# Pinning the matmuls of the 1024-column gemms in the order in which the kernel names them

## The chip, the cores and the metric

One core of a Trainium2 chip runs the whole kernel. The metric is the device time of one launch in microseconds, as the median of several runs. TensorE (PE) multiplies, VectorE (DVE) and ScalarE (ACT) prepare operands and read results out of PSUM, SyncE (SP) and GpSimd (POOL) issue the loads.

## The reference

Two transformer blocks, one after the other, on 256 tokens of width 2048 in float32. Cut to the large products:

```
# first block
h = rmsnorm(x, norm_attn); proj = h @ w_in
ya = dilated_attention(...); yb = rmsnorm(diff_attention(...))
x = x + concatenate([ya, yb]) @ w_out                      # "wo1" in the kernel
h = rmsnorm(x, norm_ffn)
x = x + (silu(h @ w_gate) * (h @ w_up)) @ w_down           # "wgu", "wd"
x = rmsnorm(x, norm_final)
# second block
z = rmsnorm(x, norm1_g) @ w_in
a_out = forgetting_attention(...)                          # "fox"
m_out = rmsnorm(mlstm_chunkwise(...)) * sigmoid(...)
merged = sigmoid(g_a) * (a_out @ w_proj_a) + sigmoid(g_m) * (m_out @ w_proj_m)   # gates: "wgs"
x = x + merged @ w_out                                     # "wo2"
u = causal_dwconv(rmsnorm(x, norm2_g) @ w_up)
x = x + (silu(u_gate) * u_val) @ w_down                    # "wd2"
```

## The kernel before

Every float32 operand is cut into a high and a low part in fp32r. Activations lie in SBUF as pairs of parts (class Pair: hi, lo), weights are loaded as 1024-column raw tiles and cut by `split` (L80): ACT casts the high part wh (L83), DVE subtracts to get the low part wl (L84). Both have four buffers, so the split of a tile waits until PE has done with the tile four before it. One product of a 128x128 piece of activations with 512 columns of weights is three matmuls, high by high, high by low, low by high, in `mm3` (L133; its matmul is L136).

`gemm` (L192) makes 256 x 1024 results in four PSUM banks c[t][col], with t the half of the tokens and col the half of the columns. It does not issue work at once: it makes a list `todo` of closures (loads, cuts, products) and runs them in order at the end. Two kinds of stage fill the list. A Plain stage takes two weight tiles; `part(h)` names, for one of them, twelve matmuls: for each 512-column half and each half of the tokens one product of three matmuls, so each goes to another of the four banks. The last Plain stage of a gemm (`by_bank`) names all products of one bank before those of the next. A Seven stage does a 2x2 block by Strassen's scheme with seven products into p1, p5, p6, p7 and c; it has four cuts (w0 to w3, of raw tiles and of the sums ta and tb) and names its products in three steps, `one` (p1, c01, c00), `two` (p5, p7, from ta) and `three` (p6, c10, from tb), between which a Plain stage's parts 0 and 1 stand. `chain` (L316) folds p1, p5, p6 and p7 together on ACT and DVE (s1 at L317, u2 at L318 and so on).

PSUM has four banks with the tag "d" and four with "a". c is in "d", except in the second wo1 gemm, where it is in "a"; p1, p5, p6 and p7 are in "a", and so are the scores of the attention (L574), the transposed probabilities (L581), the value products (L603) and the transposes of results (`turned`, L374), which DVE and ACT read out as pairs (`put`, L113 and L114; `put2`, L118 and L119).

What sets the order: the kernel names its work in one sequence, and a scheduler of the framework reorders each engine's instructions by the data they need and by times that it expects. A matmul given to `tc.keep_in_program_order` may not pass the PE instruction that was named just before it. Before the change `mm3` gets that wish only from `by_bank` of a gemm that was called with `ends` (the last one of the kernel). wo1's, wgu's, wd's, wgs's, wo2's and wd2's products go through `gemm`; the other projections (`xstat`, `wstat`), attention and transposes do not, and are never pinned.

Of the kernel before, what the change touches and what calls it, by code (L numbers as in the profile page):

```python
# [57 lines left out]
def body(ctx: ExitStack, tc: tile.TileContext, xT, xn, gfr, gp, cst, rst, w1, wo1, wgu, wd,  # L58
# [11 lines left out]
    def raw_tile(src):  # L70
        t = rp.tile([P, 1024], F32, tag="raw", name="raw")
        n = src.shape[-1]
        nc.sync.dma_start(t[:, :n], src)
        return t
# [6 lines left out]
    def split(src, n, eng=dve):  # L81
        wh, wl = wtiles()
        act.copy(wh[:, :n], src)  # L83
        eng.tensor_sub(wl[:, :n], src, wh[:, :n].bitcast(F32))  # L84
        return wh, wl

    def bank(tag="a"):
        t = psp.tile([P, 512], F32, tag=tag, name=tag)
        return t
# [44 lines left out]
    def mm3(ps, ah, al, wh, wl, start, stop, pin=False):  # L134
        for i, (a, b) in enumerate(((ah, wh), (ah, wl), (al, wh))):
            m = pe.matmul(ps, a, b, start=start and i == 0, stop=stop and i == 2)  # L136
            if pin:
                tc.keep_in_program_order(m)
# [53 lines left out]
    def gemm(srcs, xs, n_sum, fold=None, mid=None, tag="d", tail=1, lead=0, last=((0, 0), (0, 1), (1, 0), (1, 1)), ends=False):  # L192
# [13 lines left out]
        todo, count, done = [], {}, {}  # L206

        def mm(ps, lhs, w, o, pin=False):
            count[id(ps)] = count.get(id(ps), 0) + 1

            def go():
                k = done[id(ps)] = done.get(id(ps), 0) + 1
                wh, wl = w[0][:, o:o + 512], w[1][:, o:o + 512]
                mm3(ps, *lhs(), wh, wl, k == 1, k == count[id(ps)], pin)
            todo.append(go)

        def later(f):
# [2 lines left out]
        class Seven:  # L220
# [17 lines left out]
            def lhs(self, n):  # L238
                pr = xs[self.i]
                return (pr.s[:, 0, n], pr.s[:, 1, n]) if n < 4 else (pr.a(0, (n - 4) % 2, (n - 4) // 2),  # L240
                                                                     pr.a(1, (n - 4) % 2, (n - 4) // 2))
# [267 lines left out]
    with tc.tile_pool(name="a1", bufs=1) as ap1:  # L509
# [131 lines left out]
        for grp in range(4):  # L641
# [18 lines left out]
            else:  # L660
# [7 lines left out]
                for h in range(4):  # L668
                    for t in range(2):
                        dve.tensor_scalar_mul(on[:, t, h, :], on[:, t, h, :], ss[:, t, h:h + 1])  # L670
                    ps = bank()
# [87 lines left out]
    with tc.tile_pool(name="a2", bufs=1) as ap2:  # L759
# [105 lines left out]
        for w in (wmq, wmk):  # L865
            m = n4("mT")[:, 0:1024].rearrange("p (h s) -> p h s", h=4)
            for j in range(4):
                ps = bank()
# [44 lines left out]
        for j in range(4):  # L913
# [3 lines left out]
            for hf in range(2):  # L917
                ps = bank()
# [77 lines left out]
    with tc.tile_pool(name="mg", bufs=8) as mp:  # L996
        for b in range(4):
# [8 lines left out]
            for i in (1, 0):  # L1006
                for q in range(2):
                    for h in range(2):
                        wh, wl = split(raw_tile(wpr[b][i][q][:, h * 1024:(h + 1) * 1024]), 1024)
                        for kk in range(2):  # L1010
                            k = 4 * q + 2 * h + kk
# [197 lines left out]
```

## Time and profile before

| what | value |
|---|---|
| median of 3 runs | 2508.8 us (2508.21 to 2511.95) |
| the profiled execution | 2509.22 us |
| its span in the profile | 2507.4 us |
| granted TensorE clock, mean | 0.999 |
| PE, DVE, ACT busy | 2496.5, 1829.8, 1386.3 us |

In a row of the profile "d<-wh,x" means that a PSUM bank with the tag d is written from weights wh and activations x; the number after it is the tile's shape. Matmuls are pipelined, so the span of one (0.39 us for 512 columns) is longer than the distance from one start to the next.

### The profile page before, as it was taken

Reading aid. Unit: us, or ns where it says so; the run is one execution under the profiler, and the core shown is the slowest. Engines: PE = TensorE matmul, PEld = TensorE weight load, DVE = VectorE, ACT = ScalarE, POOL = GpSimd, SP = SyncE. Lnnn points to the kernel's source line nnn. Section 1 sums busy time; section 2 is a strip of 40 time slices with the busy share of each in tenths; the row PEclk is TensorE's granted clock in tenths of the full one; section 3 lists DMA queues with packets and bytes.
Section 4 is the critical chain, followed back from the end, with each engine's and each line's share of the span. In section 5 each row is a group of like instructions: output and inputs, shape, how many; then the busy total and the mean of one; then the engine's idle time right before and its main releaser. Section 6 shows DMA issues by size and latency. Waiting matters only on the chain.

```text
span 2507.4 us, 32737 instructions
## 1 busy us (share of the span) xinstructions
PE 2496.5 (100%) x11977; PEld 2080.4 (83%) x11977; DVE 1829.8 (73%) x2538; ACT 1386.3 (55%) x1943; POOL 74.1 (3%) x81
## 2 busy tenths in 40 slices
PE   9999999999999999999999999999999999999999
PEld 7888888888888888887888888888888888888887
DVE  6666567899888888886565555455788887878787
ACT  6555455665555555575456544444655555555554
POOL 0000000000000000000000000000000000000000
PEclk9999999999999999999999999999999999999999
DMA  8445566889888888866544456555756755685665
GB/s 328 151 152 170 172 203 203 255 249 271 263 250 257 259 257 246 264 199 201 189 156 160 161 191 193 192 190 186 233 189 202 249 188 186 209 260 187 187 198 170
DMA packets 159186, 528.07 MB, mean 211 GB/s; under 512 B 16688, under 2 KB 16944, under 8 KB 158768
## 3 DMA queue, kind: packets, MB, share of 16 engines
q1 hardware_dynamic: 148512, 488.75, 58.5%
q0 software_dynamic: 9936, 36.18, 8.0%
q8 instruction: 94, 1.54, 0.2%
q10 hardware_dynamic: 576, 1.05, 0.1%
q14 instruction: 68, 0.56, 0.1%
HBM read 523.81 MB, written 2.10 MB: 210 GB/s over the span
## 4 chain that ended last, share of the span: by engine, by line
PE 98%; DVE 1%; DMA 0%; issue 0%; ACT 0%; SPq 0%; DVEq 0%; ACTq 0%
PE d L136 60%; PE a L141 14%; PE a L136 12%; PE a L142 7%; PE a L374 1%; PE a L574 1%; DVE wl L84 0%; PE a L581 0%; PE d L141 0%; DMA xin<-in_xT 0%; PE a L633 0%; PE a L565 0%; PE a L603 0%; ACT wh L83 0%; PE d L142 0%
## 5 line engine op out<-in xcount | busy, mean ns | idle before, releaser
L84 DVE TENSOR_TENSOR wl<-raw,wh 128x1024 fp32r<-128x1024 f32 (+1 forms) x882 | 1037.3, 1181 | 550.1 <-ACT wh L83 546.7
L83 ACT CAST wh<-raw 128x1024 fp32r<-128x1024 f32 (+1 forms) x882 | 890.9, 1017 | 948.1 <-PE d L136 555.8
L136 PE MATMUL d<-wh,x 128*128 128x512 f32 x2932 | 926.8, 392 | 1.7 <-ACT wh L83 1.7
L136 PEld LDWEIGHTS d<-wh,x 128*128 128x128 f32 x2932 | 548.5, 188 | 115.2 <-ACT wh L83 2.8
L136 PE MATMUL d<-wl,x 128*128 128x512 f32 x1466 | 574.0, 392 | 0.9 <-DVE wl L84 0.9
L141 PE MATMUL a<-x,wh 128*128 128x512 f32 x1504 | 531.3, 399 | 0.0
L142 PE MATMUL a<-x,wl 128*128 128x256 f32 x1504 | 421.8, 281 | 0.0
L136 PE MATMUL d<-wh,y 128*128 128x512 f32 x1104 | 352.8, 391 | 0.2 <-ACT wh L83 0.2
L141 PEld LDWEIGHTS a<-x,wh 128*128 128x128 f32 x1504 | 282.4, 188 | 69.9
L136 PEld LDWEIGHTS d<-wl,x 128*128 128x128 f32 x1466 | 275.3, 188 | 59.8 <-DVE wl L84 2.9
L142 PEld LDWEIGHTS a<-x,wl 128*128 128x128 f32 x1504 | 284.1, 189 | 0.4
L136 PEld LDWEIGHTS d<-wh,y 128*128 128x128 f32 x1104 | 207.1, 188 | 43.8 <-ACT wh L83 0.6
L136 PE MATMUL d<-wl,y 128*128 128x512 f32 x552 | 213.4, 390 | 1.2 <-DVE wl L84 1.2
L136 PE MATMUL a<-wh,y 128*128 128x512 f32 x456 | 147.3, 390 | 0.4 <-ACT sv L392 0.4
L136 PEld LDWEIGHTS d<-wl,y 128*128 128x128 f32 x552 | 103.8, 188 | 23.6 <-DVE wl L84 2.0
L136 PEld LDWEIGHTS a<-wh,y 128*128 128x128 f32 x456 | 85.6, 188 | 18.9 <-ACT sv L392 0.6
L136 PE MATMUL a<-wl,y 128*128 128x512 f32 x228 | 88.6, 389 | 0.0
L84 DVE TENSOR_TENSOR wl<-ta,wh 128x1024 fp32r<-128x1024 f32 x69 | 84.2, 1221 | 4.8 <-ACT wh L83 4.6
L84 DVE TENSOR_TENSOR wl<-tb,wh 128x1024 fp32r<-128x1024 f32 x69 | 84.1, 1219 | 3.4 <-ACT wh L83 3.4
L136 PE MATMUL d<-wh,m 128*128 128x512 f32 x256 | 79.8, 391 | 0.0
L136 PE MATMUL a<-wh,sy 128*128 128x512 f32 x216 | 77.8, 393 | 0.0
L83 ACT CAST wh<-ta 128x1024 fp32r<-128x1024 f32 x69 | 72.6, 1051 | 8.8 <-PE d L136 3.9
(323 smaller groups left out, 2218.1 us busy)
## 6 DMA issues: line engine op xcount, KB each, us to landing
raw<-in_wup SPq DMA_DIRECT2D x176, 512.0 KB, 4.4
raw<-in_wgu SPq DMA_DIRECT2D x143, 512.0 KB, 6.3
raw<-in_wd SPq DMA_DIRECT2D x140, 512.0 KB, 5.5
raw<-in_w SPq DMA_DIRECT2D x95, 512.0 KB, 3.9
raw<-in_wo SPq DMA_DIRECT2D x64, 512.0 KB, 4.5
raw<-in_wgs SPq DMA_DIRECT2D x64, 512.0 KB, 4.3
raw<-in_wfox SPq DMA_DIRECT2D x48, 512.0 KB, 3.8
ta<-in_wd SPq DMA_DIRECT2D x36, 512.0 KB, 7.7
```

Source lines behind the costliest of these rows:

```text
L83: act.copy(wh[:, :n], src)
L84: eng.tensor_sub(wl[:, :n], src, wh[:, :n].bitcast(F32))
L136: m = pe.matmul(ps, a, b, start=start and i == 0, stop=stop and i == 2)
L141: pe.matmul(ps, wh, pr.t[:, :, j, :], start=start, stop=False)
L142: pe.matmul(ps[:, 0:S], wl, pr.hi(j), start=False, stop=stop)
L374: pe.transpose(ps[:, o:o + P], srcs[t][:, f:f + P], ident)
L574: pe.matmul(o, qT[lo:hi, a, h, qt * P:(qt + 1) * P], kT[lo:hi, b, h, :], start=i == 0, stop=i == 2)
```

## The change

All products that `gemm` names are now pinned, by one word in `mm`:

```diff
             def go():
                 k = done[id(ps)] = done.get(id(ps), 0) + 1
                 wh, wl = w[0][:, o:o + 512], w[1][:, o:o + 512]
-                mm3(ps, *lhs(), wh, wl, k == 1, k == count[id(ps)], pin)
+                mm3(ps, *lhs(), wh, wl, k == 1, k == count[id(ps)], True)
             todo.append(go)
```

The work is the same; on PE 3,584 of 11,864 positions hold another instruction than before, on DVE 356, on ACT 180 and on SP 15.

PE at the end of the last attention group of the first block. L581 transposes probabilities (sm), L603 multiplies them with the values; the L136 rows belong to the first wo1 gemm. Before:

```order
L136 MATMUL d_2823<-wl_2865,y_883 128x512
L581 MATMUL a_2705<-cst_t_73,sm_2712 128x128 x4
L581 MATMUL a_2733<-cst_t_73,sm_2740 128x128 x4
L136 MATMUL d_2823<-wh_2864,y_883 128x512
L136 MATMUL d_2821<-wh_2868,y_883 128x512
L136 MATMUL d_2821<-wl_2869,y_883 128x512
L136 MATMUL d_2821<-wh_2868,y_883 128x512
L136 MATMUL d_2823<-wh_2868,y_883 128x512
L581 MATMUL a_2760<-cst_t_73,sm_2767 128x128
L136 MATMUL d_2823<-wl_2869,y_883 128x512
```

PE in the same place, changed:

```order
L574 MATMUL a_2788<-kT_2541,qT_2371 128x256 x6
L581 MATMUL a_2705<-cst_t_73,sm_2712 128x128 x4
L581 MATMUL a_2733<-cst_t_73,sm_2740 128x128 x4
L603 MATMUL a_2705<-pT_2726,v_2702 128x256 x2
L581 MATMUL a_2760<-cst_t_73,sm_2767 128x128 x4
L603 MATMUL a_2733<-pT_2754,v_2702 128x256 x2
L581 MATMUL a_2788<-cst_t_73,sm_2795 128x128 x4
L603 MATMUL a_2760<-pT_2781,v_2702 128x256 x2
L603 MATMUL a_2788<-pT_2809,v_2702 128x256 x2
L136 MATMUL d_2820<-wh_2828,y_868 128x512
```

The gemm's matmuls stood among and ahead of the attention's; now all of them stand behind the last value product.

PE at the start of the second wo1 gemm, behind the transposes of the residual (L374). a_3191 to a_3194 are the four banks of its results. Before:

```order
L374 MATMUL a_3173<-cst_t_73,xin_75 128x128 x3
L136 MATMUL a_3191<-wh_3199,y_868 128x512
L136 MATMUL a_3191<-wl_3200,y_868 128x512
L136 MATMUL a_3191<-wh_3199,y_868 128x512
L136 MATMUL a_3191<-wh_3203,y_868 128x512
L136 MATMUL a_3191<-wl_3204,y_868 128x512
L136 MATMUL a_3191<-wh_3203,y_868 128x512
```

PE in the same place, changed:

```order
L136 MATMUL a_3191<-wh_3199,y_868 128x512
L136 MATMUL a_3191<-wl_3200,y_868 128x512
L136 MATMUL a_3191<-wh_3199,y_868 128x512
L136 MATMUL a_3193<-wh_3199,y_868 128x512
L136 MATMUL a_3193<-wl_3200,y_868 128x512
L136 MATMUL a_3193<-wh_3199,y_868 128x512
L136 MATMUL a_3192<-wh_3199,y_868 128x512
L136 MATMUL a_3192<-wl_3200,y_868 128x512
L136 MATMUL a_3192<-wh_3199,y_868 128x512
L136 MATMUL a_3194<-wh_3199,y_868 128x512
```

The first weight tile (wh_3199) now goes to all four banks before the second tile is used, where one bank took one tile after the other.

DVE in a wgu gemm with Seven stages, around 500 us. wl_4340 is the low part of the sum ta, wl_4318 and wl_4322 those of a Plain stage; L355 and L711 finish the results of the gemm before, L131 makes sums of a turned pair. Before:

```order
L84 TENSOR_TENSOR wl_4318<-raw_4296,wh_4317 128x1024
L355 TENSOR_TENSOR u3_4156<-d_3903,u3_4156 128x512
L131 TENSOR_TENSOR sy_4179<-sf_4174,sy_4179 128x512
L355 TENSOR_TENSOR e22_4158<-d_3904,e22_4158 128x512
L711 SCALAR_TENSOR_TENSOR s1_4154<-u4_4157,rtok_3537,s1_4154 128x512
L131 TENSOR_TENSOR sy_4197<-sf_4192,sy_4197 128x512
L84 TENSOR_TENSOR wl_4322<-raw_4298,wh_4321 128x1024
L84 TENSOR_TENSOR wl_4340<-ta_3988,wh_4339 128x1024
L711 SCALAR_TENSOR_TENSOR u3_4156<-e22_4158,rtok_3537,u3_4156 128x512
```

DVE in the same place, changed:

```order
L131 TENSOR_TENSOR sy_4179<-sf_4174,sy_4179 128x512
L355 TENSOR_TENSOR u3_4156<-d_3903,u3_4156 128x512
L711 SCALAR_TENSOR_TENSOR s1_4154<-u4_4157,rtok_3537,s1_4154 128x512
L131 TENSOR_TENSOR sy_4197<-sf_4192,sy_4197 128x512
L355 TENSOR_TENSOR e22_4158<-d_3904,e22_4158 128x512
L84 TENSOR_TENSOR wl_4318<-raw_4296,wh_4317 128x1024
L84 TENSOR_TENSOR wl_4322<-raw_4298,wh_4321 128x1024
L711 SCALAR_TENSOR_TENSOR u3_4156<-e22_4158,rtok_3537,u3_4156 128x512
L84 TENSOR_TENSOR wl_4340<-ta_3988,wh_4339 128x1024
```

The low parts moved behind the work on earlier results. On PE, in the same stage, the two high-part products with the ta tile stood together and their low-part ones some 16 matmuls later; now each product's three matmuls stand together.

## Rows read from the trace of the kernel before

**Rows 1.** The page, part 1: busy us (share of the span) xinstructions.

```profile
PE 2496.5 (100%) x11977; PEld 2080.4 (83%) x11977; DVE 1829.8 (73%) x2538; ACT 1386.3 (55%) x1943; POOL 74.1 (3%) x81
```

**Rows 2.** The chain of waits, 300 to 345 us: start us, us, what.

```profile
299.98 13.60 PE d L136 x60
...
339.35 0.86 PE a L603 x4
```

**Rows 3.** Timeline of PE there: start us, us, engine line op out<-in xcount [idle before].

```profile
313.42 3.04 PE L574 MATMUL a<-kT,qT 128*128 128x256 f32 x24
...
339.19 1.02 PE L603 MATMUL a<-pT,v 128*128 128x256 f32 x4
```

**Rows 4.** Timelines of DVE and ACT in the same stretch.

```profile
324.89 0.69 DVE L590 SCALAR_TENSOR_TENSOR sm<-a,rst_t 128x512 f32<-128x512 f32 x1 [0.58 <-PE a L581]
...
324.89 1.08 ACT L583 COPY pT<-a 128x512 f32<-128x512 f32 x2 [1.84 <-PE a L581]
...
326.80 0.52 ACT L595 ACTIVATE sm<-sm,nm 128x256 f32<-128x256 f32 x1
```

**Rows 5.** Timelines of PE and DVE at the start of the second wo1 gemm.

```profile
365.26 1.91 PE L374 MATMUL a<-cst_t,xin 128*128 128x128 f32 x16
...
375.44 0.48 DVE L114 SCALAR_TENSOR_TENSOR x<-a,gp_t,x 128x256 fp32r<-128x256 f32 x1
```

**Rows 6.** Timelines of PE and DVE between the second wo1 gemm and the first wgu gemm.

```profile
414.83 0.93 PE L374 MATMUL a<-cst_t,xin 128*128 128x128 f32 x7
...
413.75 1.23 DVE L84 TENSOR_TENSOR wl<-raw,wh 128x1024 fp32r<-128x1024 f32 x1 [0.19 <-ACT wh L83]
...
416.46 1.26 DVE L114 SCALAR_TENSOR_TENSOR x<-a,gp_t,x 128x256 fp32r<-128x256 f32 x3
```

**Rows 7.** Timelines of PE and DVE between the last two wd gemms.

```profile
1071.47 0.82 PE L374 MATMUL a<-cst_t,xin 128*128 128x128 f32 x6
...
1073.98 1.30 PE L136 MATMUL d<-wh,y 128*128 128x512 f32 x5
...
1072.10 0.88 DVE L114 SCALAR_TENSOR_TENSOR x<-a,gg,x 128x256 fp32r<-128x256 f32 x2 [0.37 <-ACT x L113]
```

**Rows 8.** Timelines of PE and DVE at the end of the fox group.

```profile
1436.58 0.38 PE L979 MATMUL a<-pT,v 128*128 128x128 f32 x2
...
1417.29 0.55 DVE L971 TENSOR_SCALAR sm<-sm,den 128x128 f32<-128x128 f32 x2
...
1422.30 0.35 DVE L958 SCALAR_TENSOR_TENSOR sm<-a,Fn,cst_t 128x128 f32<-128x128 f32 x1
```

**Rows 9.** Timelines of PE and DVE in Seven stages, wgu and wd gemms.

```profile
502.07 0.61 PE L136 MATMUL a<-wh,sx 128*128 128x512 f32 x2
...
506.15 0.39 PE L136 MATMUL a<-wl,sx 128*128 128x512 f32 x1
...
458.81 1.22 DVE L84 TENSOR_TENSOR wl<-ta,wh 128x1024 fp32r<-128x1024 f32 x1
...
500.27 0.74 DVE L711 SCALAR_TENSOR_TENSOR s<-u,rtok,s 128x512 f32<-128x512 f32 x1
500.93 0.68 DVE L131 TENSOR_TENSOR sy<-sf,sy 128x512 fp32r<-128x512 f32 x1
...
502.67 1.22 DVE L84 TENSOR_TENSOR wl<-ta,wh 128x1024 fp32r<-128x1024 f32 x1
...
562.23 0.68 DVE L318 TENSOR_TENSOR u<-a,s 128x512 f32<-128x512 f32 x1
...
946.29 1.22 DVE L84 TENSOR_TENSOR wl<-ta,wh 128x1024 fp32r<-128x1024 f32 x1
...
1029.80 1.22 DVE L84 TENSOR_TENSOR wl<-ta,wh 128x1024 fp32r<-128x1024 f32 x1
```

**Rows 10.** Busy us by stretch: PE, PEld, DVE, ACT, POOL, granted clock, DMA share, GB/s.

```profile
1943.00:1946.40 3.40, 1.61 (x5) 0.59 (x4) 3.40 (x5) 0.09 (x1) 0.00 (x0) 1.00 1.02 274
1946.40:1949.80 3.40, 2.95 (x7) 2.39 (x8) 2.19 (x4) 0.83 (x1) 0.00 (x0) 0.50 0.72 261
```

## The prediction

> **What bounds the kernel now.** I read the busy times first: over the span of 2507.4 us the matmul engine is busy for 2496.5 [rows 1], so it is idle for about 11 us in all, while VectorE stands at 73% and ScalarE at 55%. So nothing can be won but those 11 us (0.4%), and every wait that the change puts into PE's row is paid in full unless it falls where PE stands already. Next comes the price of one gemm matmul: 60 of them take 13.60 us on the chain that ended last [rows 2], 0.227 us from start to start. Five products of a high part in a row, the last four over four banks, span 1.30 us, of which 0.39 is the last one's own [rows 7]: (1.30 - 0.39) / 4 = 0.227 again. The order of the products does not by itself change their pace, and I cost the turning of hi, hi, hi, hi and then lo, lo... into hi, lo, lo bank by bank at nothing. The whole question is what arrives late. For that I read the engines' rows one stretch after another: which engine releases the matmul that now comes next, and when.
>
> **The change part by part.** The scheduler was free to let a gemm's matmuls pass transposes, attention matmuls and each other. Pinned, each stays behind the PE instruction written just before it. All times below are those of the trace; "idle" is PE time added.
>
> 1. End of the last attention group of the first block. Before, PE goes from 24 score matmuls (until 316.3) into the first wo1 gemm and fits the transposes in later and the last value products at 339.19 [rows 3]; 81 gemm matmuls, 81 x 0.227 = 18.4 us, lie between. Now none of them starts before the last value product. What remains is a chain of PE, DVE and ACT, and the weight casts that lay between its links go behind it. The fourth head's masking (0.69, at 324.89 before) and its maximum (as much) can start at about 320.9, when DVE has scaled the second head and waits for the third; with the third head's two scalings between they end at 322.8. Two exponentials of 0.52 with their sums are some 1.1, copies of two heads 1.08 [rows 4], two scalings 0.6, four transposes 0.45 (16 of the same shape span 1.91 [rows 5]), two value products 0.86 [rows 2], and the hand-overs some 0.3: the end comes at about 327.1. In these 10.8 us PE has 16 x 0.11 + 4 x 0.86 = 5.2 us of its own work: **5.6 idle**. Bounds: 4.5 if the hand-overs are shorter, 8 if some casts stay between.
>
> 2. Start of the second wo1 gemm (in the "a" banks). PE ends 16 transposes at 367.17 and then works for 48 x 0.227 = 10.9 us in the first two banks. Now the first weight tile goes to four banks in turn, and the fourth is wanted after nine matmuls, at 369.76. It is free when DVE has read a pair out of it, at 375.92 [rows 5]; the orders of DVE and ACT are the same as before in this place. **6.2 idle**, the firmest term.
>
> 3. From the second wo1 gemm to the first wgu gemm. Before, ten gemm matmuls run ahead of and among the 16 transposes, which end at 415.76, and twenty more behind them until an "a" bank is free. Now p1 comes first and waits for the fifth of DVE's reads. DVE is held by a low-part subtraction until 414.98; the reads follow at 0.40 each (three span 1.26) with two small operations among them [rows 6]: 417.4. The transposes would end at 415.76 - 10 x 0.227 = 413.4. **4.1 idle** (the reads' order might spare 1.5). The same place in the last wd gemm: with nine matmuls fewer among them the transposes end at 1072.29 - 9 x 0.227 = 1070.2; the reads start at 1072.10 and take 0.40 each [rows 7], the fifth is done at 1074.2: **4.0 idle**.
>
> 4. End of a fox attention group in the second block, where the first wgs gemm's 81 matmuls filled the place. The fourth head's masking, at 1422.30 before, can come as soon as DVE has the second head scaled, about 1417.4. Casts apart, nothing lies between that and the last value product, at 1436.58 before [rows 8], but links like those of term 1: about 6 us, so 1423.4. PE has 3.9 us of work in the 9.0 after 1414.4. **5.1 idle**, bounds 4 and 7.
>
> 5. The gemms with Seven stages (wgu and wd). Before, when a stage's ta tile was cut, its two high-part products ran at 502.07 and the low-part one not until 506.15; the split ended at 503.89 [rows 9]. Now the low part is wanted at 502.3. The scheduler moves DVE's row too: five operations of 0.60 to 0.67 stand ahead of wl_4318 that were behind it or apart, and the L711 product stands ahead of wl_4340, which so ends at about 504.5: 2.2 late, at three like places (502, 693, 946). At five like places (460 to 1031) the split is 0.18 late as it stands and 0.67 more by the L711 product: 0.85. The transposes of the turned columns wait for the chain of the Strassen sums; the worst is u2 (L318), which ends at 562.91 where the new order wants it at 560.6: 2.3 [rows 9]. Going through all 22 places between 424 and 1031 in this way: 3 x 2.2 + 5 x 0.85 + 2.3 + 1.4 + 1.5 + eleven others of 0.2 to 0.9 (6.0) = **22 idle**. Bounds: 16.6 if DVE kept the order of before, 28 if each moved split began only when its new neighbours began before.
>
> 6. The plain gemms (wgs, wo2) in their steady state: the low part is ready microseconds ahead, since ACT and DVE wait for PE to free their tiles; nothing. Without that lead each tile would cost like term 5. In the last gemms around 1943 PE already stands for 1.8 of 3.4 us [rows 10], and I add nothing there, plus or minus 1.5.
>
> 7. The clock. The granted clock fell once after the start, to 0.50 (1.2 GHz) for 3.4 us, right behind 3.4 us in which PE was busy for only 1.61 [rows 10]; half of 3.4 us of work, 1.7 us, was lost. Terms 2 and 3 leave three waits of 4 us and more that run straight into dense matmuls: 3 x 1.7 = **5.1**. Bounds 0 and 8.5.
> The Trainium skill (TensorE: Matmul & The Clock Gate, Part 1: The HAM clock gate) has an idle engine fall to half of its pulses, whatever comes after: by it terms 1 and 4 pay as well and the sum is 3.4 higher. The trace bears it out with one case only.
>
> One rule speaks against this sum: the Trainium skill (Perfetto Trace Analysis, Optimizing Tensor Performance, Matmuls) wants independent groups to rotate through PSUM banks, as the pinned order does at term 2 and the old one doesn't. By it term 2 would be nil and the sum 6.2 less. The row of DVE's read [rows 5] says the contrary here: the rotation meets a bank that isn't read out.
>
> **Sum:** 5.6 + 6.2 + 4.1 + 4.0 + 5.1 + 22 + 5.1 = 52. The profiled execution took 2509.2, the median is 2508.8; added to the first: **2561 us**.
>
> **The rivals.** (a) *Small:* only the waits at stage boundaries are real. While PE waits, DVE and ACT get ahead, and the next late split then is in time. For it speaks that DVE has a quarter of its time free; against it that its rows show no hole at the places concerned [rows 9], and that the places lie 10 us and more apart. Terms 1 to 4 alone, 25 us: 2534. (b) *Large:* the clock falls behind the waits of term 5 too, about 13 of 0.8 us and more times 1.7, 22 us: 2583. Against it: waits of that length are rare in the trace, and only two together led there. (c) *Not slower:* at 1943 to 1950 the free order itself costs PE 1.8 us of standing and 1.7 by the clock [rows 10], because it drew high parts ahead and then met several low parts in a row that DVE hadn't made; a fixed order asks for splits evenly. If that holds, and if DVE's reads move ahead of its splits so far that the boundaries are covered, the gain is those 3.5 us and less than 1 elsewhere: 2505. It decides only if the reads of terms 2 and 3 come 4 to 6 us sooner, and at term 2 the orders of DVE and ACT don't move at all. (d) The edit does nothing: excluded, 3,584 of 11,864 PE positions hold another instruction.
>
> **How the numbers follow.** Forecast 2561 with 0.58, its own range 2545 to 2575 (low: 5.4 less in term 5, 5.1 of the clock, 5 of the others; high: 6 + 3.4 + 5). Rival (a) 0.20, (b) 0.14, (c) 0.04, and 0.04 for effects that cancel to within 0.2%, which is 5 us and about what a measurement of this kernel can tell from no change. To leave no more than 2 in 10 out the range reaches to most of (a) and to just below (b): 2536 to 2580. Slower by over 0.2%: 0.92, within 0.04, faster 0.04.
>
> **What would show it.** In the profile after: PE's busy time as now and 40 to 60 us more span; among PE's waits "a" banks that wait for DVE's reads (L114), one near 6 us and two near 4; before the last value products (L603 and the fox ones) 5 us idle in pieces with no gemm matmul among them; some 20 waits for wl (L84) and a few for u2 (L318), each under 3 us; a granted clock of 0.5 for a few us behind the long ones. I am wrong if the waits for wl sum up to under 10 us (then rival a), if half clock holds for more than 15 us of busy PE (rival b), or if gemm matmuls no longer follow each other at 0.227.

## The result

| | before | changed |
|---|---|---|
| median, us | 2508.93 (4 runs) | 2548.21 (3 runs) |
| ratio, 95% interval | | 1.0157 [1.0143, 1.0171] |
| span of the profiled execution | 2507.4 | 2546.4 |
| granted TensorE clock, mean | 0.999 | 0.993 |

The change costs 39 us, 1.6%. A fourth execution of the changed kernel took 14104.5 us and is left out of its median, which is 2549.05 with it, the 2549 of the expectations below. The forecast was 2561, the range 2536 to 2580. The page of the changed kernel, part 1 (as [rows 1]), says that the engines do the same work; PE is busy for 17 us more and stands for 33 us instead of 11:

```profile
PE 2513.7 (99%) x11977; PEld 2087.8 (82%) x11977; DVE 1834.8 (72%) x2538; ACT 1391.0 (55%) x1943; POOL 74.1 (3%) x81
```

What PE waited for in the changed kernel from 20 us on (engine, line, releaser: us in total, times, longest):

```profile
PE a L136 <- DVE x L114: 12.1, 3, 4.7
PE a L581 <- DVE sm L599: 3.2, 1, 3.2
PE d L136 <- DVE xin L363: 2.8, 1, 2.8
PE a L374 <- DVE u L318: 2.0, 1, 2.0
PE a L974 <- DVE sm L971: 1.8, 1, 1.8
PE a L136 <- ACT sv L392: 1.2, 3, 0.4
PE a L978 <- ACT pT L976: 0.8, 2, 0.6
PE d L136 <- DVE wl L84: 0.7, 4, 0.2
```

Three waits for a bank that DVE reads out, each about 4 us, stand at the top, as do the links of the attention tails; the low parts (wl), for which I had foreseen some twenty waits and 22 us, hold PE for 0.7 us. This list counts only what shows as a gap: the span of a matmul is 0.39 us and the next one starts 0.227 later, so a start that is up to 0.16 us late leaves none.

A second reading places the loss. Wherever both programs have done the same set of matmuls, the start of the next common one can be compared in the two traces. The distance grows so:

| stretch (time before) | PE falls back by | foreseen |
|---|---|---|
| up to 15 us (first loads) | 0.9 | 0 |
| end of the last attention group, to 340 | 5.6 | 5.6 |
| start of the second wo1 gemm, to 379 | 7.7 | 6.2, and clock 1.7 |
| second wo1 to first wgu gemm, to 424 | 6.8 | 4.1, and clock 1.7 |
| all the Seven stages, 424 to 1004 | 5.7 | 22 |
| between the last wd gemms, to 1082 | 6.7 | 4.0, and clock 1.7 |
| end of the fox group, to 1437 | 5.6 | 5.1 |
| all the rest | 0.0 | 0 |

The sum is 39, the difference of the spans. The first row is not the change's: no gemm of this kind runs there, and by the same comparison the runs below lie between -0.6 and 2.5 us. The first long wait and what follows it, in PE's timeline of the changed kernel (as [rows 5]):

```profile
377.18 0.40 PE L136 MATMUL a<-wh,y 128*128 128x512 f32 x1
...
382.32 0.77 PE L136 MATMUL a<-wh,y 128*128 128x512 f32 x1 [4.75 <-DVE x L114]
382.89 0.63 PE L136 MATMUL a<-wl,y 128*128 128x512 f32 x1
383.32 1.05 PE L136 MATMUL a<-wh,y 128*128 128x512 f32 x2
```

The fourth product waits 4.75 us for DVE's read, and from there one matmul follows the other at 0.43 us, not 0.227. The stretches of the three waits and of the gemms behind them (busy us of PE, PEld, DVE, ACT, POOL, then granted clock, DMA share, GB/s):

```profile
377.50:382.10 4.60, 0.08 (x1) 0.00 (x0) 3.51 (x11) 4.44 (x13) 0.00 (x0) 0.71 0.09 37
382.10:386.10 4.00, 3.78 (x9) 3.03 (x10) 1.72 (x3) 1.04 (x1) 0.00 (x0) 0.50 0.00 0
427.50:431.30 3.80, 0.18 (x2) 0.00 (x0) 3.62 (x10) 3.78 (x11) 0.00 (x0) 0.91 0.44 135
431.30:437.30 6.00, 5.88 (x14) 4.65 (x15) 3.16 (x6) 3.75 (x5) 0.00 (x0) 0.50 0.13 46
1096.90:1100.60 3.70, 0.21 (x2) 0.00 (x0) 3.52 (x8) 3.70 (x11) 0.00 (x0) 0.87 0.40 128
1100.60:1106.30 5.70, 5.56 (x13) 4.43 (x14) 2.39 (x4) 2.37 (x3) 0.00 (x0) 0.50 0.19 60
316.90:327.50 10.60, 7.42 (x33) 5.68 (x32) 7.88 (x21) 7.40 (x23) 0.00 (x0) 0.84 0.15 54
1447.20:1456.50 9.30, 6.71 (x28) 4.49 (x26) 6.75 (x26) 5.79 (x19) 0.00 (x0) 0.82 0.16 56
```

Behind each of the three waits the granted clock is 0.50 (1.2 GHz) for 4.0, 6.0 and 5.7 us of gemm: half of that, 2.0, 3.0 and 2.9 us, is lost work, 7.9 in all. In the two attention tails (the last rows) the clock is low for part of the time as well; it is back before the gemm begins, but it makes the tails themselves longer, as the section on the prediction shows.

### The profile page after: what moved, and what is told of

Read it like the earlier page. It is cut to its first block, busy times and chain, and to the rows that moved or that the text cites. A ratio compares the mean times of both kernels' runs of the same rounds, so it can differ in the third digit from the quotient of the medians.

```text
span 2546.4 us, 32739 instructions
## 1 busy us (share of the span) xinstructions
PE 2513.7 (99%) x11977; PEld 2087.8 (82%) x11977; DVE 1834.8 (72%) x2538; ACT 1391.0 (55%) x1943; POOL 74.1 (3%) x81
## 4 chain that ended last, share of the span: by engine, by line
PE 95%; DVE 3%; issue 1%; ACT 1%; DMA 0%; SPq 0%; DVEq 0%; ACTq 0%
PE d L136 57%; PE a L141 14%; PE a L136 12%; PE a L142 7%; DVE wl L84 1%; PE a L374 1%; PE a L574 1%; ACT wh L83 0%; PE a L581 0%; PE a L603 0%; PE d L141 0%; PE a L633 0%; PE a L565 0%; DMA raw<-in_w 0%; PE a L978 0%
## 5 line engine op out<-in xcount | busy, mean ns | idle before, releaser
L136 PE MATMUL d<-wh,x 128*128 128x512 f32 x2932 | 936.4, 393 | 2.3 <-ACT wh L83 2.3
L136 PEld LDWEIGHTS d<-wh,x 128*128 128x128 f32 x2932 | 550.2, 188 | 116.6 <-ACT wh L83 3.2
L136 PE MATMUL d<-wl,x 128*128 128x512 f32 x1466 | 575.1, 392 | 0.8 <-DVE wl L84 0.8
L136 PE MATMUL d<-wh,y 128*128 128x512 f32 x1104 | 360.2, 392 | 2.8 <-DVE xin L363 2.8
L136 PEld LDWEIGHTS d<-wl,x 128*128 128x128 f32 x1466 | 276.2, 188 | 61.6 <-DVE wl L84 4.0
L136 PEld LDWEIGHTS d<-wh,y 128*128 128x128 f32 x1104 | 208.7, 189 | 46.7 <-issue 3.2
L136 PE MATMUL d<-wl,y 128*128 128x512 f32 x552 | 216.0, 391 | 0.2 <-DVE wl L84 0.2
L136 PE MATMUL a<-wh,y 128*128 128x512 f32 x456 | 150.0, 395 | 9.6 <-DVE x L114 8.4
L136 PEld LDWEIGHTS d<-wl,y 128*128 128x128 f32 x552 | 104.5, 189 | 22.7 <-DVE wl L84 0.8
L136 PEld LDWEIGHTS a<-wh,y 128*128 128x128 f32 x456 | 86.8, 190 | 29.5 <-issue 9.0
L136 PE MATMUL a<-wl,y 128*128 128x512 f32 x228 | 89.7, 393 | 0.0
L136 PE MATMUL d<-wh,m 128*128 128x512 f32 x256 | 79.5, 390 | 0.0
L136 PE MATMUL a<-wh,sy 128*128 128x512 f32 x216 | 77.5, 390 | 0.0
```

## The experiments

The questions were: are these costs local, and do they add up; is it the pin against other stages or the order within a gemm; does the half clock come from PE's standing; and why did the Seven stages cost so little. "Changed" is the changed kernel, with the median 2548.2; each ratio is against the kernel before in the same comparison. "Falls back" is meant as in the table above.

**One part of the change alone.** `gemm` gets an argument `hold` in place of the constant, and the calls named set it:

```diff
-                mm3(ps, *lhs(), wh, wl, k == 1, k == count[id(ps)], True)
+                mm3(ps, *lhs(), wh, wl, k == 1, k == count[id(ps)], hold or pin)
```

The two wo1 gemms only. Expected:

> Only the two wo1 gemms are pinned. Between the traces of before and after, PE falls back by 5.6 us over the end of the last attention group and by 7.7 us over the start of the second wo1 gemm. If the costs are local waits that add up, this kernel takes 2508.9 + 13.3 = 2522 us, and the wait ahead of the first wgu gemm is gone. If a wait at one place only moves a loss that would come later anyway (DVE and ACT get ahead and give it back in the Seven stages), it stays under 2516.

Measured 2524.0 us (2520.9 to 2526.4), ratio 1.0060 [1.0044, 1.0077]: 15 us over before, as local waits have it. The first wgu gemm, unpinned here, doesn't wait: PE is busy for 12.00 of the 12 us behind 424, at full clock.

The Seven stages without the long waits (wgu but the first, wd but the very last):

> Pinned are the wgu gemms but the first and the wd gemms but the very last: the Seven stages without the long waits at the boundaries. Theory A (the late splits are mild because the pinned order also finishes the banks that DVE waits for earlier, so DVE starts earlier): the 5.7 us that the changed kernel lost between 424 and 1004 us show here too, 2514 to 2515. Theory B (DVE and ACT got ahead during the long waits, which hid the late splits; my 22 us were right by themselves): 2525 to 2531.

Measured 2517.05 us (2513.2 to 2518.2), ratio 1.0030 [1.0019, 1.0041]: 7.5 us by the ratio, some 2 us over what theory A foresaw and far from theory B. In its trace the Seven stretch falls back 6.0 us, the first loads 1.3 and the place at 1943, which is not pinned here, 1.5. Theory B, the reason that I had given for rival (a), falls: without any boundary wait ahead of them the late splits cost no more. In the Seven stretch (440 to 1090 us) the waits of this kernel and, in the second fence, of the changed one are alike:

```profile
PE a L374 <- DVE u L318: 2.0, 1, 2.0
PE d L136 <- DVE wl L84: 0.5, 3, 0.2
```

```profile
PE a L374 <- DVE u L318: 2.0, 1, 2.0
PE d L136 <- DVE wl L84: 0.5, 3, 0.2
```

The second block only (wgs, wo2, wd2):

> Only the gemms of the second block are pinned (wgs, wo2, wd2). By local waits that add up: the end of the fox group, 5.6 us, and nothing else, 2514.5. If the plain stages or the last gemms cost anything that the trace of the changed kernel hides, more than 2516; if the attention tail is made up later, under 2511.

Measured 2515.23 us (2513.5 to 2515.9), ratio 1.0022 [1.0012, 1.0031]: 5.5 us by the ratio, 6.2 by the medians; the fox tail falls back 4.9 in its trace. By their ratios the three parts add up to 15 + 7.5 + 5.5 = 28; the two gemms that no part had pinned, with 6.8 and 6.7 us in the table, make it 41.5, and the whole change is 39. With intervals of 1 to 2 us on each part that is the same.

**Pinned among themselves, free against the rest.** The first product of each gemm is not pinned, all others are:

```diff
         def mm(ps, lhs, w, o, pin=False):
+            pin = len(named) > 0
+            named.append(ps)
...
-                mm3(ps, *lhs(), wh, wl, k == 1, k == count[id(ps)], True)
+                mm3(ps, *lhs(), wh, wl, k == 1, k == count[id(ps)], pin)
```

> All is pinned but the first product of each gemm, so that a gemm may move ahead as a whole and only its own order is fixed. By local waits: both attention tails (5.6 + 5.6) are filled again, the three waits for an a bank stay: 2549 - 11.2 = 2538. If it is the gemm's own order that costs most, it stays at 2546 or above; if the pin against other stages is all of it, 2515 or less.

Measured 2536.91 us (2535.9 to 2537.5), ratio 1.0110 [1.0095, 1.0125]: 11.3 us less than the changed kernel. The gemm moves into the attention tails again as a whole, the L581 and L974 waits are gone, and the three bank waits stay exactly as they were. PE's waits in this kernel:

```profile
PE a L136 <- DVE x L114: 12.1, 3, 4.7
PE d L136 <- DVE xin L365: 3.0, 1, 3.0
```

**The three bank waits.** In the first Seven stage, p1's product is named behind the Plain stage's part 0, in every gemm:

```diff
             def one(self):
                 later(lambda: self.cut(0, self.r[0], 1024))
-                mm(p1, lambda: self.lhs(4), self.w[0], 0)
+                if self.i > 0:
+                    self.first()
...
                 pl.part(0)
+            if i == 0:
+                sv.first()
             sv.two()
```

> All pinned as in the change, but in the first Seven stage of each gemm the product p1 is named behind the Plain stage's part 0, 18 matmuls (4.1 us) later. If the waits ahead of the first wgu and the last wd gemm come from p1's bank being still read (3.9 and 3.8 us in the trace after, and half clock behind them, 2.9 us each), both go nearly whole: 2549 - 13 = 2536, and the granted clock stays at full there. If something else holds these gemms back (a late split, a load), 2545 or more.

Measured 2549.2 us (2547.3 to 2550.9), ratio 1.0158 [1.0139, 1.0176]: no gain at all, against 13 expected. But the two waits did shrink, from 3.7 and 3.6 us to 0.9 and 1.0: PE is busy for 11.07 of the 12 us from 424 on, at full clock. The loss came back elsewhere: the Seven stretch falls back 12.9 us instead of 5.7, and the last gemms 3. Waits in the Seven stretch, 440 to 1090 us:

```profile
PE d L136 <- DVE wl L84: 6.7, 15, 0.9
PE a L380 <- DVE u L324: 1.9, 1, 1.9
```

The new naming wants the Plain stage's low parts three matmuls, 0.68 us, sooner, and now fifteen waits for wl come up, 6.7 us, where there were three with 0.5. So the low parts had less than 0.7 us to spare in the pinned order: they were nearly late, as I had thought, and not late. The same edit in the two gemms alone where p1's bank is late:

```diff
+                if self.i > 0 or not p1_late:
+                    self.first()
...
+            c, p = gemm(wgu[gi], xr, N_SUM, lambda p: p, run_late, p1_late=gi == 0)
```

> All pinned as in the change, p1 named 18 matmuls later in two gemms alone, the first wgu gemm and the very last wd gemm. In the run that did so in all gemms the waits at these two places fell from 3.9 + 2.9 and 3.8 + 2.7 us (standing and half clock) to 1.1 each, and waits of 0.5 to 1.0 us for low parts came up in the other gemms. If that is why the whole did not get faster, this kernel takes 2549 - 11 = 2538 us. If the gain at a boundary is lost again behind it whatever the other gemms do, 2546 or more.

Measured 2535.64 us (2534.2 to 2537.3), ratio 1.0107 [1.0093, 1.0121]: 12.6 us less than the changed kernel. In its trace the two boundaries fall back 1.2 and 1.5 us, 10.7 less than before this edit, as expected; the rest is at places that it doesn't touch. Where the long wait is removed without wanting other things sooner, both the standing and the half clock are saved.

In the second wo1 gemm, the products of the first two stages named bank by bank:

```diff
+            if banks and i < banks:
+                if i == 0:
+                    pair_ = tails[:banks]
+                continue_ = i < banks - 1
+                if not continue_:
+                    for t, col in last:
+                        for q in pair_:
+                            for h in range(2):
+                                j = col if h == 0 else 1 - col
+                                mm(c[t][col], lambda j=j, t=t, q=q: q.lhs(j, t), q.w[h], j * 512)
+            elif i == len(tails) - 1:
```

> All pinned as in the change, but the first two stages of the second wo1 gemm name their products bank by bank, the fourth bank 36 matmuls (8.2 us) after the start instead of 9. If the wait there is for that bank's readers, 7.7 us with its half clock go: 2541.3. If the wait moves to another place (the first bank must then have four splits in time), 2546 or more.

Measured 2539.56 us (2538.7 to 2540.2), ratio 1.0120 [1.0104, 1.0136]: 8.7 us less than the changed kernel; the start of this gemm no longer falls back at all (7.7 before). The same stretch, by windows, has neither a long hole nor a slow clock:

```profile
371.00:376.00 5.00, 4.60 (x29) 3.86 (x28) 4.19 (x7) 4.12 (x8) 0.00 (x0) 1.00 0.32 102
376.00:384.00 8.00, 7.95 (x36) 6.30 (x35) 6.48 (x18) 6.70 (x17) 0.00 (x0) 1.00 0.32 117
```

**The clock.** Additional matmuls, whose result nothing uses, fill the three waits:

```diff
+                if fill and n == fill[0]:
+                    for _ in range(fill[1]):
+                        tc.keep_in_program_order(pe.matmul(idle, lhs()[0], wh, start=True, stop=True))
                 mm3(ps, *lhs(), wh, wl, k == 1, k == count[id(ps)], True)
```

> All pinned as in the change; in the three waits for an a bank PE runs 20, 16 and 15 additional matmuls whose result is never used (4.5, 3.6 and 3.4 us at 0.227). They end before the banks come free, so by themselves they cost nothing. If the half clock behind these waits comes from PE standing there, it disappears: 2.0 + 3.0 + 2.9 = 7.9 us of the time, 2541. If the clock falls for another reason, 2549 or a little more.

Measured 2541.25 us (2540.7 to 2542.6), ratio 1.0128 [1.0112, 1.0144]: 7.0 us less for 51 matmuls more. The rows of the stretches that answer to the three above:

```profile
378.00:382.50 4.50, 4.50 (x22) 3.70 (x21) 3.41 (x11) 4.50 (x14) 0.00 (x0) 1.00 0.19 74
382.50:386.50 4.00, 3.78 (x17) 2.84 (x16) 2.40 (x4) 1.49 (x2) 0.00 (x0) 1.00 0.00 0
426.50:430.80 4.30, 4.23 (x21) 3.25 (x20) 4.12 (x11) 4.28 (x11) 0.00 (x0) 1.00 0.42 132
430.80:436.00 5.20, 5.20 (x24) 4.28 (x24) 3.66 (x7) 3.62 (x6) 0.00 (x0) 1.00 0.15 55
1094.00:1099.20 5.20, 5.20 (x33) 4.40 (x31) 4.71 (x8) 5.20 (x13) 0.00 (x0) 1.00 0.51 181
1099.20:1105.00 5.80, 5.60 (x26) 4.48 (x25) 4.02 (x7) 2.90 (x5) 0.00 (x0) 1.00 0.27 89
```

In the same 4.0 us behind the first wait PE now does 17 matmuls, not 9. The half clock there does come from PE standing, and it is the only thing that the fill took away: the bank comes free no sooner, as DVE's read of it starts 10.2 us after the start of the transposes in both kernels.

**All the repairs together**, first with p1 late in all gemms, then in two:

> Pinned, but with the first product of each gemm free, p1 late and the second wo1 gemm's start bank by bank. If the five places are the whole cost but for the Seven stages: 2549 - 11.2 - 13 - 7.7 = 2517, and 5 to 6 us of that against before are the Seven stages'. If the costs replace each other, 2525 or more; if the free order of before was itself no better, 2511 or less.

Measured 2533.99 us (2531.6 to 2534.8), ratio 1.0096 [1.0080, 1.0112]: 17 too much. Its waits for wl are those of the first p1 experiment, 6.7 us in fifteen; the next kernel, which differs in that edit alone, takes 12.5 us less, so about twelve of the 17 were that edit's own.

> The pinned order with the first product of each gemm free, the second wo1 gemm's first stages bank by bank, and p1 late in the two gemms alone. If the five places add up: 2549 - 11.2 - 9.5 - 11 = 2517, and what is left against before is the Seven stages' 5.7 and some 2 at the two boundaries. If they replace each other, 2525 or more.

Measured 2521.52 us (2520.4 to 2526.6), ratio 1.0049 [1.0034, 1.0064], 4.5 us over the sum of the single gains. Of the 39 us 26.7 go with the five places and 12.5 are left. Its trace, of the longest of the four executions (2526.6), says where some of them are: p1 meets its bank still 1.7 us too early here, since the gemm begins earlier, and the clock falls again behind it:

```profile
418.00:423.50 5.50, 2.69 (x10) 1.68 (x9) 4.68 (x11) 5.30 (x10) 0.00 (x0) 0.86 0.57 181
423.50:429.00 5.50, 5.50 (x14) 4.24 (x14) 3.25 (x5) 0.62 (x1) 0.86 (x1) 0.52 0.67 107
```

So the places do replace each other a little: this boundary falls back 6.4 us in that trace, where p1 named late alone left 1.2. The rest is the Seven stages (8.3) and the boundary between the last wd gemms (2.0); the gemms behind 1437 cost nothing.

**Why the Seven stages cost little.** In the kernel before, the four banks of a wgu gemm end nearly together, in the changed one one after the other, and DVE may begin to read early. With the last Plain stage of wgu and wd left free this spread is mostly undone:

```diff
-        def mm(ps, lhs, w, o, pin=False):
+        def mm(ps, lhs, w, o, pin=True):
...
-                        mm(c[t][col], lambda j=j, t=t: self.lhs(j, t), self.w[h], j * 512, ends)
+                        mm(c[t][col], lambda j=j, t=t: self.lhs(j, t), self.w[h], j * 512, not tail_free)
```

> All pinned as in the change but the last Plain stage of the wgu and wd gemms, whose matmuls the scheduler may order. In the changed kernel that stage finishes its four banks one after another (positions 2076, 2082, 2088, 2094 on PE in the first wgu gemm), in the kernel before nearly at once (2087, 2089, 2091, 2094), in this one at 2084, 2086, 2088, 2094, with DVE's order as in the changed kernel. Theory: DVE reads the early banks 1.8 to 2.5 us sooner, in what was a hole, and that is why the late splits cost 5.7 us and not 22; then this kernel's splits come 0.25 us later where DVE has a hole left and 1 us or more at the three places where it has none, 4 to 8 us in all: 2553 to 2557. If the splits are in time for another reason, 2548 to 2550.

Measured 2549.82 us (2546.9 to 2550.7), ratio 1.0153 [1.0139, 1.0167]: the same as the changed kernel within the noise. The 4 to 8 us did not come in the times. Its trace falls back 9.2 us in the Seven stretch, not 5.7, but 1.6 of the difference is a half clock behind the wait for u2. DVE begins to read the banks 1.8 us ahead of the last bank's last matmul, not 3.65, and the split of ta ends 5.37 us behind that matmul, not 5.19: 0.2 us later, as foreseen for the places with a hole left, but at the three places without one nothing changed. So the earlier reads are not what puts the splits in time at those three; at the five a part of them is left here (the kernel before began to read 1.16 us ahead), so for these the run decides nothing. What the rows show stands in the next section.

**The other side.** The free order loses about 4 us at 1943 to 1949, by standing and at half clock [rows 10]. In the kernel before, four additions of that gemm moved from DVE to GpSimd:

```diff
-            dve.tensor_add(r, c[t][n], r)
+            eng.tensor_add(r, c[t][n], r)
...
+    lambda p, g=g: add_blocks(p, g, eng=pool if part == 0 and g == 0 else dve)
```

> The kernel before, unpinned, with one more edit: in the first part's first wd2 gemm the four additions of folded results to the residual run on GpSimd instead of DVE. DVE is late with four low parts at 1943 to 1947 there, and PE stands for 2.6 us and loses 1.5 more at half clock. If DVE's queue is the reason, 2.4 us of work leave it and the time falls by 2 to 4 us, to 2505 to 2507; if the loads or ACT hold the place, no change, 2509; if DVE then waits for GpSimd's slower additions (1.79 us each on such tiles), 2510 or more.

Measured 2507.1 us (2505.75 to 2511.3) beside 2509.05, ratio 0.9994 [0.9985, 1.0003], at the upper end of the foreseen 2505 to 2507. The place is mended in the profile:

```profile
1938.00:1942.00 4.00, 3.02 (x13) 2.18 (x13) 4.00 (x7) 2.10 (x2) 1.85 (x3) 1.00 0.92 259
1942.00:1946.00 4.00, 3.96 (x16) 2.47 (x14) 4.00 (x4) 1.80 (x2) 3.25 (x2) 1.00 1.03 335
1946.00:1950.00 4.00, 3.74 (x17) 2.96 (x17) 3.96 (x6) 0.31 (x1) 0.00 (x0) 1.00 0.62 211
```

One wait of 1 us is left, the clock stays at full, and the span is 2504.4, 3 us less; the times can't tell that from no change with certainty. No kernel tried is surely faster than the one before.

## Why the prediction was right, and where it was wrong

- **The total** lies in the range partly by luck. The range reached down to 2536 to take in rival (a), and the largest term of the sum, 22 of 52 us, was wrong by 16. Two of the signs of being wrong that I had named came true: the waits for wl sum up to 0.7 us, under 10, and half clock holds for 15.2 us of busy PE behind the three waits alone, just over 15. The second was to speak for rival (b); its cause, falls behind the waits of term 5, is not in this trace.
- **The bound** held: the 11 us in which PE stood were all that could be won, and the waits and the slow clock that came on went into the time, 39 us of span.
- **Terms 1 and 4**, the attention tails: 5.6 and 5.6 measured for 5.6 and 5.1. Leaving the first product free gave back 11.3 us for the two (expected 11.2), so it is the pin against the other stage, not the order within the gemm. The closeness of the sizes is partly luck: the measured ones hold half clock, which the two terms left out. From the start of the last score matmuls (L956) to the first matmul of the gemm the fox tail takes 10.01 us in the changed kernel, and 8.27 and 9.01 in the kernels with p1 late in two gemms and in all, where the clock stayed at full there, so by these some 1.0 to 1.7 of the 5.6 are the clock's. The tail in the first of these two (columns as in the stretches above):

```profile
1436.80:1445.10 8.30, 5.79 (x33) 4.08 (x31) 6.52 (x26) 5.67 (x19) 0.00 (x0) 1.00 0.18 63
```

- **Terms 2 and 3**: the standing was 4.75 and twice 0.42 us, then 3.7 and 3.6, for 6.2, 4.1 and 4.0. One sentence of term 2 was a slip without effect: before the change PE worked in three banks, for 36 matmuls or 8.2 us, until the fourth was free, not in two for 48. The Trainium skill (Perfetto Trace Analysis, Optimizing Tensor Performance, Matmuls) wants independent groups to rotate through banks. At this place the runs say otherwise: naming it bank by bank made it 8.7 us faster than rotating. Behind the fox tail, where the pinned gemms rotate through their banks too, PE falls back by nothing in all.
- **Term 5 is the step that failed**: 22 foreseen, 5.7 measured, and of the 22 late places only u2's (2.0) had its size. Counted from start to start, 49 matmuls of the stretch come over 0.05 us late, 8.7 us in all, where 28 did by 3.6; but for u2's none is over 0.33. I took the time at which DVE ended a split before, moved it by the operations that now stand ahead of it, and compared it with the new time of use. That holds DVE's start fixed. DVE's rows of before, ahead of the places that I looked at, have long holes:

```profile
453.48 0.69 DVE L355 TENSOR_TENSOR s<-d,s 128x512 f32<-128x512 f32 x1 [2.51 <-PE d L136]
...
485.46 0.69 DVE L318 TENSOR_TENSOR u<-a,s 128x512 f32<-128x512 f32 x1 [2.02 <-PE a L136]
```

  and the same operations in the changed kernel, with two of PE: the last matmul of the gemm's last bank (475.61) and the first use of ta's low part (480.85):

```profile
471.96 0.69 DVE L355 TENSOR_TENSOR s<-d,s 128x512 f32<-128x512 f32 x1
473.32 0.69 DVE L355 TENSOR_TENSOR u<-d,u 128x512 f32<-128x512 f32 x1 [0.67 <-PE d L136]
...
475.61 0.39 PE L136 MATMUL d<-wh,x 128*128 128x512 f32 x1
...
476.04 0.69 DVE L355 TENSOR_TENSOR e<-d,e 128x512 f32<-128x512 f32 x1 [0.57 <-PE d L136]
...
479.58 1.22 DVE L84 TENSOR_TENSOR wl<-ta,wh 128x1024 fp32r<-128x1024 f32 x1
...
480.85 0.50 PE L136 MATMUL a<-wl,sx 128*128 128x512 f32 x1
...
504.40 1.22 DVE L84 TENSOR_TENSOR wl<-raw,wh 128x1024 fp32r<-128x1024 f32 x1
506.59 0.69 DVE L318 TENSOR_TENSOR u<-a,s 128x512 f32<-128x512 f32 x1 [0.98 <-PE a L136]
...
523.01 1.22 DVE L84 TENSOR_TENSOR wl<-ta,wh 128x1024 fp32r<-128x1024 f32 x1
```

  Counted from the last matmul of the gemm's last bank, DVE's first addition (L355) starts 3.65 us ahead, where it started 1.16 ahead before, and a split stands in the hole ahead of u2. At the five like places the split of ta so ends 5.19 us behind that matmul and is wanted at 5.24: in time by 0.05, not late by 0.85. The p1 experiment shows how near it was: wanted 0.68 us sooner, 15 of the places are late.

  At the three places without a hole it is the split that moved into the hole ahead of u2. From the start of u2 to the end of ta's split DVE takes 18.4 us before (485.46 to 503.89) and 17.6 in the changed kernel (506.59 to 524.23), with one more L711 product between the two but one split fewer. The kernel with the last stage left free, where the reads are later, has the split in the hole too, and the same 17.6:

```profile
504.71 1.23 DVE L84 TENSOR_TENSOR wl<-raw,wh 128x1024 fp32r<-128x1024 f32 x1
507.05 0.69 DVE L318 TENSOR_TENSOR u<-a,s 128x512 f32<-128x512 f32 x1 [1.11 <-PE a L136]
...
523.47 1.22 DVE L84 TENSOR_TENSOR wl<-ta,wh 128x1024 fp32r<-128x1024 f32 x1
```

  At the five others the earlier reads make up for the L711 product. Both are readings of rows; no run undoes the one or the other alone.
- **Rival (a)** had the direction of this error, but not its reason: that DVE gets ahead during the long waits is refuted by the kernel without them. Its evidence against, no hole at the places concerned, looked at the rows of the places and not at those ahead of them.
- **Term 7** had the right cause, as the fill shows, and too small a size: 5.1 foreseen, 7.9 measured. I priced each fall with the 3.4 us of [rows 10], 1.7 us of work; here the half clock lasted 4.0 to 6.0 us of gemm. The Trainium skill's rule (TensorE: Matmul & The Clock Gate, Part 1: The HAM clock gate), that an idle engine falls whatever comes after, agrees with the tails too (0.84 and 0.82 granted). It cost no gemm there, but time of the tails, as told above.
- **Rivals (b) and (c)**: behind the 2 us wait for u2 the clock stayed at full in the changed kernel's trace; no gain of the even order is seen at 1943 either, where PE now waits 2.8 us for another addition and falls to half clock in this trace.

The total was too high by 13 us: term 5 by 16 and the standing of terms 2 and 3 by 1, while term 7, the first loads and the tails had 4 too little.

## What to carry to other kernels

A fixed order within a gemm cost this kernel 6 to 8 us; nearly all the rest came from five seams, where a product named early needed a bank that another engine was still reading, or where a pin kept independent work from filling a chain of three engines. So free the first product of each stage, and name first what needs no bank of the stage before. When you move an instruction on paper, move the whole queue that feeds it: look at the holes ahead of the place before you call an operation late.

## What the runs showed of the hardware that I had not expected

The price of a wait at half clock is not fixed by the wait. Behind the same wait for u2, about 2 us, the traces of two kernels that are alike at this place differ: it left the clock at 1.00 in the changed kernel and brought it to half in the filled one (mean 0.57 over the 4 us behind it):

```profile
584.60:590.00 5.40, 5.32 (x26) 4.48 (x27) 5.40 (x9) 1.64 (x2) 0.87 (x1) 1.00 1.00 283
```

```profile
582.00:586.00 4.00, 4.00 (x12) 3.15 (x11) 4.00 (x6) 0.32 (x1) 0.86 (x1) 0.57 1.04 254
```

The first row is of the changed kernel, the second of the one with the filled waits. Over all the traces of the pinned kernels this wait cost nothing or 1.7 us of work, and a bank wait of 3.6 to 4.8 us cost 1.5 to 3.1 on top of the standing. One kernel's own executions differ too: the last kernel with all repairs had a mean granted clock of 0.997, 0.999, 1.0 and 0.999 in times of 2526.6, 2521.6, 2520.4 and 2521.5 us. A single trace therefore does not give the price of a wait.
